# A fifth Strassen pair in the second mixer of a decoder trunk, with a new order of segments and new tables for it

## The chip, the cores and the metric

The kernel runs on one core of one Trainium2 chip. The metric is device time in microseconds of one execution, median over runs; smaller is better. The engines named below are PE (matrix multiplications; PEld is its weight load), DVE (vector), ACT (scalar and activation), POOL and SP (here both used to issue DMAs).

## The reference, cut to what matters

Two layers over 256 rows of 2048 float32 values. Each layer has an attention part and a channel mixer; the mixer, with the norm around it, is what the change touches:

```python
def swiglu(h, w_in, w_out):
    gate, up = jnp.split(h @ w_in, 2, axis=-1)
    return (jax.nn.silu(gate) * up) @ w_out
...
        h = modulate(rms_norm(x, norm_g[layer, 2]), sh2, sc2)
        y = swiglu(h, ffn_w_in[layer], ffn_w_out[layer])
        x = x + g2[:, None, :] * rms_norm(y, norm_g[layer, 3])
```

`w_in` is 2048 x 11264 (gate and up, 5632 columns each), `w_out` 5632 x 2048, and `g2` a vector of 2048 that is itself a product of the condition `c` with a 2048 x 2048 piece of `mod_w`.

## The kernel before

**Products.** Every float32 product is made of three matmuls in the fast `float32r` type: a weight block `raw` (512 x 512, held as 128x2048) is copied in rounded form by ACT (`wh`), DVE subtracts that from the original to get the remainder (`wl`), and PE adds hh·wh, hh·wl and hl·wh into a PSUM bank, where hh and hl are the two parts of the data. A *unit* is one weight block against one half t (128 rows) of the data: 12 matmuls of 128x512. The 5632 inner values are 11 blocks of 512, the 2048 outputs are 4 blocks `nb`.

**A planner.** The Python program keeps its own clock for each engine (`Emit`) and emits instructions when, by its own costs, their inputs will be there: the units stand in a fixed list, weight preparation (`w_load2`, `st_load`) and all epilogues are put between them by the planner. The result is one fixed order per engine; at run time each engine takes its instructions in that order and waits on semaphores. `TUNE` has one row of settings per stage (how many blocks to load ahead, `RAW`; how many prepared weights to keep, `AHEAD` and `MOST`; leads and lateness of preparation and of epilogues); its last row is that of the second mixer. `AT1` is the table of places at which the 16 loads of the last piece of `mod_w` are put among the weight loads. Where the planner expects PE to stand for more than 1.2 (`FILL_MIN`) with a bank free, `fill` emits small matmuls of the identity into a spare bank (`idle`).

**Strassen pairs.** `PAIRS` says how many pairs of inner blocks of each mixer (here one in the first, four in the second) go by Strassen's algorithm in its form with seven products. For a pair p of inner blocks and a pair c of output blocks, the two halves of the rows and the two inner blocks make a 2x2 matrix, which is multiplied by the 2x2 matrix of weight blocks X, Y, W, Z (`st_load`). Plainly that is eight units; here it is seven products, in the order of `ST_ORDER`:

```python
    ST_ADD = {"Q5": ("X", "Y"), "P6": ("X", "Z"), "P7": ("Y", "Z"), "P4": ("X", "W")}
    ST_ORDER = ("P1", "Q5", "P6", "P7", "P3", "P2", "P4")
```

Four of the seven need a weight that DVE first sums in place (`rawX`, `rawY`), and each needs a `wh` and a `wl` of its own. On the data's side `ep_up` keeps the transposed activations of a pair in `fT` (besides their split form `fa`), and `combine` makes the four sums and differences and splits them into `Sh` and `Sl`. After each product `st_out` adds the bank (`sacc`) to the partial output `yp`, on DVE for all pairs but the first.

**Order of the second mixer.** `SEGS` lists, for each mixer, segments of inner blocks: for each block 4 x 2 units of the gate part (`acc` from `hhF`, then `sg` by ACT's Silu) and as many of the up part (DVE multiplies into `sg`, PE transposes into `aT`, ACT and DVE make `fa`). One pair of units, t = 0 and t = 1, shares a weight block. A tuple (p, a, b) in a segment spreads the 14 products of pair p evenly over places a to b in the segment's list of such pairs of units. `LASTK` lists the inner blocks of the last pass: for each output block and each half, `y_block` adds that pass's `acc` to `yp`, ACT sums the squares (`junk`), DVE multiplies by the gate row `G`; `residual` then takes the root (`stat`) and updates X, which goes out. G is a vector of `mod` turned into a row by `gate_rows`: a transposition (`gT`), a copy, a DMA to memory (`grow`) and one back, both on POOL's queue; X comes back from memory by POOL's queue behind it (`x_in`).

Of the kernel before, what the change touches and what calls it, by code (L numbers as in the profile page):

```python
# [50 lines left out]
FILL_FROM = 24.0  # L51
FILL_MIN = 1.2
FILL_LEAVE = 0.7
PAIRS = (1, 4)
W0 = 24
SEGS = (((range(0, 2), (), ()), (range(2, 6), ((0, 3, W0),), range(2, 6)), (range(6, 11), (), ())),
        ((range(0, 2), (), ()), (range(2, 11), ((0, 3, 16), (1, 19, 32), (2, 35, 48), (3, 51, 71)), ())))
LASTK = (range(6, 11), range(8, 11))
ATM = (6, 10, 10, 13, 18, 21, 22, 23, 24, 25, 26, 28, 30, 31, 39, 41, 46, 52, 55, 58, 61, 61, 62, 64, 65, 67, 68, 70,
# [5 lines left out]
AT1 = (1, 4, 4, 4, 6, 7, 33, 46, 60, 73, 95, 112, 115, 126, 139, 149)  # L65

NAMES = ("RAW", "AHEAD", "MOST", "LAG", "LAGX", "LAGR", "T1_LEAD", "URGENT", "LEADS", "BIAS", "ST_RAW", "ST_AHEAD", "XLATE", "LATE", "MLATE", "RLATE")
TUNE = tuple(dict(zip(NAMES, row)) for row in (
# [4 lines left out]

C_ID, C_NTRI, C_ANY, C_NEG1, C_ONE, C_LO, C_HI, C_KEEP = 0, 128, 256, 258, 259, 260, 261, 262
C_MASK, C_MASKT, C_CMP, C_COS, C_SIN, C_END = 262, 390, 518, 550, 806, 1062
# [455 lines left out]
def kernel(ctx: ExitStack, tc, consts, x, c, mod_w, mod_b, norm_g, ffn_w_in, ffn_w_out, a_w_in,  # L531
# [8 lines left out]
    E = Emit(nc)  # L540
# [68 lines left out]
    def cols(n):  # L609
        nstat[0] += n  # L610
        return stat[:, nstat[0] - n:nstat[0]]
# [212 lines left out]
    def w_load2(key, src):  # L824

        st = {}
        view = lambda tl: tl.rearrange("p (j n) -> p j n", j=4)

        def dma():
            st["t"] = E.alloc("pg", "raw")  # L830
            DMA.dma_start(view(st["t"]), src.rearrange("(j p) n -> p j n", p=P))

        def first():
            st["h"] = E.alloc("pg", "wh", R32)
            st["l"] = E.alloc("pg", "wl", R32)
            A.activation(st["h"], st["t"], AF.Copy)

        def second():
            V.tensor_tensor(st["l"], st["t"], st["h"].bitcast(F32), op=OP.subtract)
            E.put("pg", st["t"])  # L840
            E.ready[key] = (view(st["h"]), view(st["l"]), E.fin)

        return Load(key, "w", 2, dma, lambda: E.when(st["t"]), first, second, mid=lambda: E.when(st["h"]))
# [6 lines left out]
    ST_ORDER = ("P1", "Q5", "P6", "P7", "P3", "P2", "P4")  # L850
# [109 lines left out]
    def sumsq(src, acc):  # L960
        j = yield from E.get("s2", "junk")
        A.activation(j, src, AF.Square, accum_out=acc)
        E.put("s2", j)
# [129 lines left out]
    gate_keys = ["A", "F0", "B", "F1"]  # L1093
    PAGED = ["A", "B"] + [f"F{l}" for l in range(2) if PAIRS[l]]
    NEXT = [k for k in ("A", "F0", "B") if gate_keys[gate_keys.index(k) + 1] in PAGED]
# [37 lines left out]
    def y_block(key, nb, t, acc, part=None):  # L1133

        yield from E.wait((key, "G"))
        if nb == 0:
            res[key, t, "ss"] = cols(4)
            res[key, t] = part[t] if part else (yield from E.get("pg", "z"))
        while (key, t) not in res:
            yield False  # L1140
        z = res[key, t][:, nb * NB:(nb + 1) * NB]
        Gb = res[key, "G"][:, nb * NB:(nb + 1) * NB]
        if part:
            V.tensor_tensor(z, acc, z, op=OP.add)
            E.put("mm", acc)
            src = z
        else:
            src = acc
        if part and nb == KT - 1:
            z = res[key, t, "last"] = yield from E.get("s2", "zl")  # L1150
        yield from sumsq(src, res[key, t, "ss"][:, nb:nb + 1])
        V.tensor_tensor(z, src, Gb, op=OP.mult)
        if not part:
            E.put("mm", acc)
        E.flag((key, "y", t, nb))
# [555 lines left out]
    def ep_up(acc, key, blk, t):  # L1711
# [12 lines left out]
        src = b  # L1724
        if blk < 2 * PAIRS[int(key)]:
            src = L["fT" + key, blk, t] = yield from E.get("s2", "fT")
# [7 lines left out]
    def combine(key, p):  # L1734

        yield from E.wait(*[("f" + key, 2 * p + i, t) for i in range(2) for t in range(2)])
        sh = yield from E.get("pg", "Sh", R32)
        sl = yield from E.get("pg", "Sl", R32)
        if p == 0:
            for t in range(2):  # L1740
                ypart[key, t] = yield from E.get("pg", "yp")
        q = [L["fT" + key, 2 * p + i, t] for i in range(2) for t in range(2)]
        v = lambda tl: tl.rearrange("p (q j n) -> p q j n", q=4, j=4)
        sh, sl = v(sh), v(sl)
        flat = lambda tl, i: tl[:, i].rearrange("p j n -> p (j n)")
        for o, a, b, op in ((3, 1, 3, OP.subtract), (1, 0, 1, OP.subtract), (0, 3, 0, OP.subtract), (2, 2, 0, OP.add)):
            V.tensor_tensor(q[o], q[a], q[b], op=op)
            A.activation(flat(sh, o), q[o], AF.Copy)
        yield E.clk["DVE"] - 1.0
        for o in (3, 1, 0, 2):  # L1750
            V.tensor_tensor(flat(sl, o), q[o], flat(sh, o).bitcast(F32), op=OP.subtract)
            E.put("s2", q[o])
        L["S" + key, p] = sh, sl
        E.flag(("S" + key, p))
# [47 lines left out]
    def mm_units(seg, W, col0, nb, kts, lhs, epi, tag="mm"):  # L1802

        us = []
        for i, kt in enumerate(kts):
            key = (seg, nb, kt)
            wsrc[key] = W[kt * NB:(kt + 1) * NB, col0:col0 + NB]
            us.append([dict(kind="mm", key=key, t=t, lhs=(lhs, kt), acc=(seg, nb, t), start=i == 0,
                            stop=i == len(kts) - 1, epi=epi, tag=tag, nb=nb) for t in range(2)])
        return us  # L1810

    def call(fn):
        units.append(dict(kind="call", fn=fn))
# [87 lines left out]
    def ffn_pairs(l, key, gvec, nxt, final):  # L1901
# [7 lines left out]

        for p in range(PAIRS[l]):  # L1910
            call(lambda p=p: E.spawn(combine(key, p)))
# [26 lines left out]
        for nb in range(4):  # L1938
            us = mm_units("y" + key, wo, nb * NB, nb, LASTK[l], fl,
                          lambda a, t, nb_: y_block("F" + key, nb_, t, a, part()))  # L1940
            if nb == 2:
                call(lambda: E.spawn(x_in("F" + key)))
            if nb < 3:
                emit_plain(us)
            else:
                emit_lag(us)

    def ffn_units(l, key, gvec, nxt, final=False):
        if PAIRS[l]:
            return ffn_pairs(l, key, gvec, nxt, final)  # L1950
        lhs = "hF" + key
        fl = "f" + key
        wi, wo = ffn_w_in[l], ffn_w_out[l]

        def in_block(b):
            g = mm_units("g" + key, wi, b * NB, b, range(4), lhs, lambda a, t, nb: ep_gateff(a, key, nb, t))
            u = mm_units("u" + key, wi, DFF + b * NB, b, range(4), lhs, lambda a, t, nb: ep_up(a, key, nb, t))
            return g, u

        for b in range(FB1):  # L1960
            g, u = in_block(b)
            if b == 0:
                emit_lag(g)
                reserve(row("AHEAD"))
            else:
                emit_plain(g)
            emit_plain(u)
        for nb in range(4):
            emit_plain(mm_units("p" + key, wo, nb * NB, nb, range(FB1), fl, lambda a, t, nb_: ep_part(a, key, nb_, t)))
        for b in range(FB1, NFB):  # L1970
            g, u = in_block(b)
            emit_plain(g)
            emit_plain(u)
        reserve(row("LAG") + row("LAGR"))
        part = lambda: [ypart[key, 0], ypart[key, 1]]
        call(lambda: [E.spawn(gate_rows("F" + key, gvec))]
             + [E.spawn(residual("F" + key, t, nxt, final)) for t in range(2)])
        for nb in range(4):
            us = mm_units("y" + key, wo, nb * NB, nb, range(FB1, NFB), fl,
                          lambda a, t, nb_: y_block("F" + key, nb_, t, a, part()))  # L1980
            if nb < 3:
                emit_plain(us)
            else:
                emit_lag(us)
# [31 lines left out]
    def mods_of(vecs):  # L2016
        return [("mod", v, k) for v in vecs for k in range(16)]
# [12 lines left out]
    def placed(ks, mods, at):  # L2030
        assert len(at) == len(mods) and max(at) <= len(ks)
        return [k for i in range(len(ks) + 1) for k in [m for m, a in zip(mods, at) if a == i] + ks[i:i + 1]]
# [14 lines left out]
    ms = mods_of([(1, 5)])  # L2047
    order += placed(ks, ms, AT1)

    for k in order:  # L2050
# [10 lines left out]
        elif k[0] == "st":  # L2061
            E.loads.append(st_load(k))
        elif k in k0[:TWO] or k[0][:-1] in ("g", "u", "y") and PAIRS[int(k[0][-1])]:
            E.loads.append(w_load2(k, wsrc[k]))
# [173 lines left out]
```

## Time and profile before

| | |
|---|---|
| median of 3 runs | 2348.44 us (2348.31 to 2349.58) |
| profiled execution | 2348.64 us, span 2346.9 us |
| PE busy | 2310.0 us, 98% of the span |
| PEld busy | 1880.6 us, 80% |
| DVE busy | 1878.4 us, 80% |
| ACT busy | 1114.1 us, 47% |
| DMA | 672.23 MB, mean 286 GB/s |
| granted PE clock, mean | 0.998 |
| chain that ended last | PE 93%, DVE 2%, ACT 2%, DMA 2% |

Busy time is an average over stages; a stage's own window and its rows tell what it waits for. Matmuls are pipelined, so that the time from one start to the next, not the duration of one, is what a matmul takes. All compute instructions have the line of the recording helper (L130), so rows are told apart by tiles: `sacc` are the Strassen products, `acc` the plain units, `raw` with X, Y, Z or W the weight blocks of a pair. The second mixer runs from 1627.5 us to the end; its last matmul ends at 2338.7.

### The profile page before, as it was taken

Reading aid. Unit: us, or ns where it says so; the run is one execution under the profiler, and the core shown is the slowest. Engines: PE = TensorE matmul, PEld = TensorE weight load, DVE = VectorE, ACT = ScalarE, POOL = GpSimd, SP = SyncE. Lnnn points to the kernel's source line nnn. Section 1 sums busy time; section 2 is a strip of 40 time slices with the busy share of each in tenths; the row PEclk is TensorE's granted clock in tenths of the full one; section 3 lists DMA queues with packets and bytes.
Section 4 is the critical chain, followed back from the end, with each engine's and each line's share of the span. In section 5 each row is a group of like instructions: output and inputs, shape, how many; then the busy total and the mean of one; then the engine's idle time right before and its main releaser. Section 6 shows DMA issues by size and latency. Waiting matters only on the chain.

```text
span 2346.9 us, 27100 instructions
## 1 busy us (share of the span) xinstructions
PE 2310.0 (98%) x10967; PEld 1880.6 (80%) x10967; DVE 1878.4 (80%) x1557; ACT 1114.1 (47%) x1194; POOL 13.1 (1%) x28
## 2 busy tenths in 40 slices
PE   6999999999999999999999999999999999999998
PEld 4678787888888888888888888888888888888887
DVE  4878789997877778877878768886868888888774
ACT  3433555563444334334455355765445445454442
POOL 0000000000000000000000000000000000000000
PEclk9999999999999999999999999999999999999999
DMA  9998977989467999989779979977825666574592
GB/s 352 387 392 308 360 263 292 374 305 338 172 233 279 382 339 389 352 329 333 286 275 337 344 260 363 322 271 274 314 92 204 233 215 233 192 256 164 203 333 107
DMA packets 267646, 672.23 MB, mean 286 GB/s; under 512 B 12672, under 2 KB 30336, under 8 KB 240384
## 3 DMA queue, kind: packets, MB, share of 16 engines
q1 hardware_dynamic: 263808, 649.13, 76.3%
q0 software_dynamic: 3008, 21.01, 2.3%
q8 instruction: 86, 1.41, 0.2%
q10 hardware_dynamic: 704, 0.36, 0.1%
q14 instruction: 40, 0.33, 0.0%
HBM read 662.03 MB, written 8.42 MB: 286 GB/s over the span
## 4 chain that ended last, share of the span: by engine, by line
PE 93%; DVE 2%; ACT 2%; DMA 2%; issue 1%; SPq 0%; DVEq 0%; ACTq 0%
PE acc L130 77%; PE sacc L130 8%; PE sc L130 2%; PE z L130 1%; DVE wl L130 1%; PE oT L130 1%; DMA modq<-in_mod_w_dram 1%; PE aT L130 1%; ACT junk L130 1%; PE pmod L130 1%; PE qacc L130 1%; PE hT L130 1%; ACT hf L130 1%; DMA modw<-in_mod_w_dram 0%; PE cs L130 0%
## 5 line engine op out<-in xcount | busy, mean ns | idle before, releaser
L130 DVE TENSOR_TENSOR wl<-raw,wh 128x2048 fp32r<-128x2048 f32 (+1 forms) x349 | 786.3, 2260 | 169.8 <-ACT wh L130 157.4
L130 ACT ACTIVATE wh<-raw 128x2048 fp32r<-128x2048 f32 (+1 forms) x349 | 658.7, 1893 | 517.0 <-PE acc L130 226.3
L130 PE MATMUL acc<-wh,hhF 128*128 128x512 f32 x2816 | 889.5, 391 | 0.0
L130 PEld LDWEIGHTS acc<-wh,hhF 128*128 128x128 f32 x2816 | 528.5, 188 | 111.4 <-issue 1.7
L130 PE MATMUL acc<-wl,hhF 128*128 128x512 f32 x1408 | 548.0, 389 | 0.0
L130 DVE SCALAR_TENSOR_TENSOR macc<-modw,cact,macc 128x2048 f32<-128x2048 f32 x180 | 422.6, 2348 | 47.2 <-DMA modw<-in_mod_w_dram 37.8
L130 PEld LDWEIGHTS acc<-wl,hhF 128*128 128x128 f32 x1408 | 264.5, 188 | 53.7 <-DVE wl L130 0.2
L130 PE MATMUL acc<-wh,fa 128*128 128x512 f32 x768 | 241.0, 391 | 0.0
L130 PE MATMUL acc<-wh,hA 128*128 128x512 f32 x640 | 220.3, 404 | 1.5 <-DVE hA L130 1.5
L130 PEld LDWEIGHTS acc<-wh,fa 128*128 128x128 f32 x768 | 144.2, 188 | 32.4 <-issue 2.5
L130 PE MATMUL acc<-wh,hhK 128*128 128x512 f32 x512 | 161.2, 392 | 0.4 <-DVE hhK L130 0.4
L130 ACT ACTIVATE wh<-rawX 128x2048 fp32r<-128x2048 f32 x40 | 76.6, 1915 | 156.5 <-DVE rawX L130 137.3
L130 PEld LDWEIGHTS acc<-wh,hA 128*128 128x128 f32 x640 | 120.2, 188 | 37.6 <-issue 13.8
L130 PE MATMUL acc<-wl,fa 128*128 128x512 f32 x384 | 149.6, 390 | 0.0
L130 PE MATMUL acc<-wl,hA 128*128 128x512 f32 x320 | 125.5, 392 | 3.4 <-DVE wl L130 3.4
L130 DVE TENSOR_TENSOR wl<-rawX,wh 128x2048 fp32r<-128x2048 f32 x40 | 91.6, 2290 | 37.9 <-ACT wh L130 37.6
L130 PEld LDWEIGHTS acc<-wh,hhK 128*128 128x128 f32 x512 | 96.0, 188 | 21.2 <-issue 0.8
L130 PE MATMUL acc<-wl,hhK 128*128 128x512 f32 x256 | 99.8, 390 | 0.3 <-DVE wl L130 0.3
L130 PE MATMUL acc<-wh,hhB 128*128 128x512 f32 x256 | 86.5, 400 | 0.0
L130 PE MATMUL acc<-wh,oA 128*128 128x512 f32 x256 | 85.3, 399 | 0.0
L130 PEld LDWEIGHTS acc<-wl,fa 128*128 128x128 f32 x384 | 72.1, 188 | 14.8 <-DVE wl L130 0.3
L130 PE MATMUL acc<-wh,oB 128*128 128x512 f32 x256 | 82.4, 394 | 0.0
(228 smaller groups left out, 2507.6 us busy)
## 6 DMA issues: line engine op xcount, KB each, us to landing
raw<-in_ffn_w_in_dram SPq DMA_DIRECT2D x176, 1024.0 KB, 6.7
modw<-in_mod_w_dram SPq DMA_DIRECT2D x160, 1024.0 KB, 7.0
raw<-in_ffn_w_out_dram SPq DMA_DIRECT2D x48, 1024.0 KB, 7.5
raw<-in_a_w_in_dram SPq DMA_DIRECT2D x40, 1024.0 KB, 14.2
modq<-in_mod_w_dram SPq DMA_DIRECT2D x32, 1024.0 KB, 14.1
modw<-in_kv_mod_w_dram SPq DMA_DIRECT2D x32, 1024.0 KB, 7.5
raw<-in_kv_w_dram SPq DMA_DIRECT2D x32, 1024.0 KB, 9.1
raw<-in_a_w_out_dram SPq DMA_DIRECT2D x16, 1024.0 KB, 8.5
```

Of the source, the lines that this page charges most:

```text
L130: return f(*a, **k)
```

## The change

A fifth pair of inner blocks (8 and 9) of the second mixer goes by the seven products. `LASTK` falls from three blocks to one, block 10. In `SEGS` the products of pairs 0 to 3 stand in narrower stretches (11 places each), and those of pair 4 in places 65 to 71, among the up units of block 9 and the units of block 10. `y_block` is emitted only after all products of its output pair. `AT1` and the last row of `TUNE` have new values.

```diff
-PAIRS = (1, 4)
+PAIRS = (1, 5)
...
-        ((range(0, 2), (), ()), (range(2, 11), ((0, 3, 16), (1, 19, 32), (2, 35, 48), (3, 51, 71)), ())))
-LASTK = (range(6, 11), range(8, 11))
+        ((range(0, 2), (), ()), (range(2, 11), ((0, 3, 14), (1, 19, 30), (2, 35, 46), (3, 51, 62), (4, 65, 71)), ())))
+LASTK = (range(6, 11), range(10, 11))
...
-AT1 = (1, 4, 4, 4, 6, 7, 33, 46, 60, 73, 95, 112, 115, 126, 139, 149)
+AT1 = (1, 4, 4, 4, 12, 19, 32, 39, 44, 60, 72, 83, 87, 101, 103, 122)
...
-    (6, 2, 5, 6, 2, 0, 3, (9, 3, 0), (8.0, 0, 10.0), (-0.9, 0.2, -1.0), 4, 4, (0.3, 0.6), 3.8, 0.5, 0.7)))
+    (6, 2, 4, 6, 2, 0, 3.5, (9, 7, 0), (19.0, 19.0, 24.0), (-0.5, 0.2, -0.9), 4, 4, (0.4, 0.9), 1.6, 0.5, 1.5)))
...
     def y_block(key, nb, t, acc, part=None):
 
         yield from E.wait((key, "G"))
+        if part:
+            l = int(key[1])
+            yield from E.wait(*[("so" + key[1], p, nb // 2, nm) for p in range(PAIRS[l]) for nm in ST_ORDER])
```

Up to the second mixer the order of every engine is that of before. Within it, three places are shown. First DVE, where it prepares the second column pair of the last pair of blocks. Before (that pair is the fourth) the rows from the first product's weight to the third's are, with `raw` without a letter a plain block:

```order
L130 TENSOR_TENSOR wl_15252<-rawX_15203,wh_15251 128x2048
L130 TENSOR_TENSOR wl_15283<-raw_15215,wh_15282 128x2048
L130 TENSOR_TENSOR rawX_15203<-rawX_15203,rawY_15243 128x2048
L130 TENSOR_TENSOR wl_15313<-rawX_15203,wh_15312 128x2048
L130 TENSOR_TENSOR yp_12284<-yp_12284,sacc_15316 128x512
L130 TENSOR_TENSOR wl_15331<-raw_15289,wh_15330 128x2048
L130 TENSOR_TENSOR rawX_15203<-rawX_15203,rawZ_15338 128x2048
L130 TENSOR_TENSOR yp_12300<-yp_12300,sacc_15363 128x512
L130 TENSOR_TENSOR wl_15377<-rawX_15203,wh_15376 128x2048
```

and now (the fifth):

```order
L130 TENSOR_TENSOR wl_15801<-rawX_15726,wh_15800 128x2048
L130 TENSOR_TENSOR yp_12272<-yp_12272,sacc_15635 128x512
L130 TENSOR_TENSOR rawX_15726<-rawX_15726,rawY_15728 128x2048
L130 TENSOR_TENSOR wl_15839<-rawX_15726,wh_15838 128x2048
L130 TENSOR_TENSOR rawX_15726<-rawX_15726,rawZ_15808 128x2048
L130 TENSOR_TENSOR yp_12271<-yp_12271,sacc_15858 128x512
L130 TENSOR_TENSOR yp_12272<-yp_12272,sacc_15879 128x512
L130 TENSOR_TENSOR wl_15875<-rawX_15726,wh_15874 128x2048
L130 TENSOR_TENSOR rawY_15728<-rawY_15728,rawZ_15808 128x2048
L130 TENSOR_TENSOR wl_15893<-raw_15823,wh_15892 128x2048
```

The plain splits that stood between the summed ones are gone from these rows.

Second PE at the third product (P6) of that column pair. Before it is followed and preceded by plain units without a filler; now:

```order
L130 MATMUL sacc_15879<-wh_15838,Sl_15594 128x512
L130 LDWEIGHTS identb
L130 MATMUL idle_15901<-identb 128x256
...
L130 MATMUL sacc_15858<-wh_15874,Sh_15593 128x512
L130 LDWEIGHTS identb
L130 MATMUL idle_15911<-identb 128x256
...
L130 MATMUL sacc_15858<-wl_15875,Sh_15593 128x512
L130 MATMUL sacc_15858<-wh_15874,Sl_15594 128x512
```

Eight fillers stand ahead of P6's first matmul and thirteen ahead of its second, which is the first to read `wl`; nine stand behind the first matmul of the next plain unit, and nine in the last pass. The second mixer had none before.

Third PE where the last pass begins, `hhF` being block 10's up units and `fa` the activations of a block. Before (three blocks in that pass):

```order
L130 MATMUL acc_15628<-wh_15702,hhF_1769_11586 128x512
L130 MATMUL acc_15795<-wh_15721,fa_15069 128x512
L130 MATMUL acc_15795<-wl_15722,fa_15069 128x512
...
L130 MATMUL aT_15815<-K,sg_15595 128x128 x4
L130 MATMUL acc_15823<-wh_15721,fa_15069 128x512
...
L130 MATMUL aT_15839<-K,sg_15613 128x128 x4
L130 MATMUL acc_15795<-wh_15739,fa_15439 128x512
```

and now (block 10 alone):

```order
L130 MATMUL acc_15845<-wh_16042,hhF_1769_11586 128x512
L130 MATMUL gT_16122<-K,mall 16x128
L130 MATMUL aT_16129<-K,sg_15773 128x128 x4
L130 MATMUL acc_16137<-wh_16058,fa_16134 128x512
L130 MATMUL acc_16137<-wl_16059,fa_16134 128x512
...
L130 MATMUL aT_16157<-K,sg_15791 128x128 x4
L130 MATMUL acc_16168<-wh_16058,fa_16134 128x512
```

Before, the two transpositions of block 10 stood among units of earlier blocks; now the unit behind the first of them reads what it makes, and the gate row's `gT` stands just ahead of it. On DVE the last pass has the same rows but one order: the four updates of X for t = 0 stand directly ahead of the last add of t = 1 in both, with one unit of PE between the two halves' last matmuls instead of three.

## The prediction

> **What bounds the kernel now.** I read the page's head, then the stretch of the second mixer as one window, then the chain that ended last, then DVE and ACT in order of time where the change puts its new work.
>
> ```profile
> span 2346.9 us, 27100 instructions
> PE 2310.0 (98%) x10967; PEld 1880.6 (80%) x10967; DVE 1878.4 (80%) x1557; ACT 1114.1 (47%) x1194; POOL 13.1 (1%) x28
> PE 93%; DVE 2%; ACT 2%; DMA 2%; issue 1%; SPq 0%; DVEq 0%; ACTq 0%
> 1627.50:2338.70 711.20, 711.08 (x3190) 587.00 (x3188) 564.04 (x401) 342.95 (x264) 2.66 (x5) 1.00 0.61 217
> 1867.73 5.44 PE sacc L130 x24
> ```
>
> The window from 1627.5 to 2338.7 is the second mixer, from its first matmul to its last: columns are PE, PEld, DVE, ACT, POOL, then the granted clock 1.00. PE is busy 711.08 of 711.20 us, so in this stage it waits for nothing, and a matmul taken out there is worth its full spacing. The row of the chain gives that: 24 matmuls take 5.44 us, 0.2267 us each; a unit (12 matmuls, one block against one half of the rows) takes 2.72 us. DVE is busy 79% of the stage. So every microsecond that PE learns to wait here is lost as fully as a matmul is won.
>
> **What is removed.** Two units of eight go to seven products for each of two column pairs: 24 matmuls, 5.44 us. Nothing else can be won in this stage, since there is no wait to take away. The profiled execution took 2348.64 us, 1.7 us more than its span; the median of the runs is 2348.44, so the same sum from either differs by 0.2 us.
>
> By the Trainium skill, "TensorE: Matmul & The Clock Gate", section Back-to-back issue gap, matmuls of 512 columns in a stream with weight loads come about 131 ns apart, by which the 24 would be worth about 3.1 us (an estimate). The row has 227 ns; the measurement decides.
>
> **What is added, on DVE and ACT.** The durations, in order of time:
>
> ```profile
> 2085.64 2.28 DVE L130 TENSOR_TENSOR rawX<-rawX,rawW 128x2048 f32<-128x2048 f32 x1
> 2089.96 2.29 DVE L130 TENSOR_TENSOR wl<-rawX,wh 128x2048 fp32r<-128x2048 f32 x1 [2.04 <-ACT wh L130]
> 2092.17 0.68 DVE L130 TENSOR_TENSOR yp<-yp,sacc 128x512 f32<-128x512 f32 x1
> 2092.77 2.28 DVE L130 TENSOR_TENSOR wl<-raw,wh 128x2048 fp32r<-128x2048 f32 x1
> ...
> 2103.36 0.43 DVE L130 CAST fa<-fT 128x512 fp32r<-128x512 f32 x1
> 2103.82 0.69 DVE L130 TENSOR_TENSOR fa<-fT,fa 128x512 fp32r<-128x512 f32 x1
> 2104.43 2.29 DVE L130 TENSOR_TENSOR wl<-raw,wh 128x2048 fp32r<-128x2048 f32 x1
> 2106.63 2.86 DVE L130 TENSOR_TENSOR fT<-fT,fT 128x512 f32<-128x512 f32 x4
> 2109.41 2.35 DVE L130 SCALAR_TENSOR_TENSOR macc<-modw,cact,macc 128x2048 f32<-128x2048 f32 x1
> 2111.67 2.49 DVE L130 TENSOR_TENSOR Sl<-fT,Sh 128x512 fp32r<-128x512 f32 x4
> 2114.08 2.29 DVE L130 TENSOR_TENSOR wl<-rawX,wh 128x2048 fp32r<-128x2048 f32 x1
> ```
>
> From start to start: a 128x2048 instruction takes 2.20 us, a 128x512 one 0.60, a cast 0.46, the four of combine's sums 2.78, its four remainders 2.41. The first two rows show the weak spot: a product with a summed weight needs an add on DVE, the rounded copy `wh` on ACT, then the remainder `wl` on DVE, and DVE stands 2.04 us for ACT if it has nothing in between.
>
> A pair trades 8 weight splits for 14 and adds 8 sums, so 14 instructions of 2.20 us more, about 31 us of DVE, with combine's 5.2 and the output sums on top. Blocks two to four have it in cycles of 46 units, 125 us of PE, and there DVE has, counted in the order, 30 splits, 8 sums, 2 to 4 `macc` (2.26 us), 6 to 14 output sums and some 20 small ones: by these rows 106 to 112 us in the new order against 103 to 108 before, beside PE as today. The `macc` of the last gate vector now all come in these cycles, none behind them: they add to the 112, and take 2.26 us each out of what follows. I cost the narrower bunches (11 pairs instead of 13 for 14 products) at nothing, covered by the five pairs of plain units behind each; 3 us if that cover fails.
>
> The fifth pair has no such rest behind it. I walk DVE's new order from T0, the end of the second transposition of block 9 (aT into PSUM), by those durations. DVE reaches the work of that half at T0+1.3: it has two products with `sg`, one add, a copy, a cast, a remainder and a split (7.45 us together) from the last-but-one unit of block 9, while PE has two units and two transpositions (6.15 us). From there to the remainder that block 10's first half needs stand 29 instructions of 2.20 (63.8 us) and 16.6 us of small ones (two of a cast, 2.78, 2.41, 14 output sums, two `sg`, one more). DVE also stands behind the add, copy, remainder sequence six times, with whatever small work is left to fill it: 1.2 + 0.35 (the first of them for P1's end on PE), 1.5, 2.1, 2.1, 0.9 and 1.5 us, 9.65 in all. 1.3 + 63.8 + 16.6 + 9.65: that remainder ends at T0+91.3.
>
> PE has 29 units up to there, 78.9 us, one small transposition and block 10's first aT, then two matmuls before the one that needs the remainder:
>
> ```profile
> 2273.18 0.60 PE L130 MATMUL aT<-K,sg 128*128 128x128 f32 x4
> ...
> 2273.54 0.48 PE L130 MATMUL acc<-wh,fa 128*128 128x512 f32 x1
> ...
> 2274.77 0.60 ACT L130 ACTIVATE fa<-aT 128x512 fp32r<-128x512 f32 x1 [2.42 <-DVE wl L130]
> ```
>
> That is 78.9 + 0.1 + 0.36 + 0.45 = T0+79.75 if PE never waits. PE waits 11.7 us, by the walk 0.35 before P6, 1.2 P7, 0.7 P4 and 0.1 the next unit (column pair 0), 1.2 before Q5, 1.7 and 2.05 at P6, 1.7 in the unit behind it (column pair 1), 0.7 for ACT's `fa` and 2.0 for its remainder. The second half adds 0.4: 12.1 us. Before, block 10's aT went under four units of blocks 8 and 9 that the last pass had first; now that pass has block 10 alone.
>
> The 39 filler matmuls that now stand at four of these places are no more than part of the waits. Alone they would cost:
>
> ```profile
> 1236.74 2.58 PE L130 MATMUL idle<-identb 128*128 128x256 bf16 x22
> ```
>
> 0.117 us each, 4.6 us, even if PE would not have waited.
>
> **The end.** The last output block of each half of the rows:
>
> ```profile
> 2319.69 0.69 DVE L130 TENSOR_TENSOR yp<-acc,yp 128x512 f32<-128x512 f32 x1 [5.81 <-PE acc L130]
> 2321.18 0.69 DVE L130 TENSOR_TENSOR yp<-yp,G 128x512 f32<-128x512 f32 x1 [0.79 <-ACT junk L130]
> ...
> 2324.50 0.15 DVE L130 TENSOR_REDUCE stat<-stat 128x1 f32<-128x3 f32 x1
> ...
> 2324.94 0.15 DVE L130 TENSOR_SCALAR stat<-stat 128x1 f32<-128x1 f32 x1
> ...
> 2330.57 0.69 DVE L130 TENSOR_TENSOR yp<-acc,yp 128x512 f32<-128x512 f32 x1 [5.48 <-PE acc L130]
> ...
> 2334.57 0.75 DVE L130 SCALAR_TENSOR_TENSOR X<-zl,stat,X 128x512 f32<-128x512 f32 x1
> 2338.73 0.69 DVE L130 TENSOR_TENSOR yp<-acc,yp 128x512 f32<-128x512 f32 x1 [3.41 <-PE acc L130]
> ```
>
> From the first half's last add to the end of its four updates of X DVE needs 4.75 us; three units, 8.16 us, lay between the two halves, so the second never met the first. Now one unit, 2.72 us, lies between, and the four small sums of `stat` (0.6 us from the first to the last's end) fall into the same place, in front of the square root: the second half starts 5.3 us behind the first instead of 2.7, 2.6 us later.
>
> The gate row G comes late:
>
> ```profile
> 2288.24 0.50 POOL L130 DMA_DIRECT2D grow<-grow  x1 [650.61 <-ACT grow L130]
> 2293.77 0.56 POOL L130 DMA_DIRECT2D G<-grow  x1 [5.02 <-DMA raw<-in_ffn_w_out_dram]
> ...
> 2298.80 0.69 DVE L130 TENSOR_TENSOR yp<-yp,G 128x512 f32<-128x512 f32 x1 [3.91 <-DMA G<-grow]
> ```
>
> 10.6 us from its first DMA to its use. The new order issues it when the last pass begins, about T0+88.9, so the first output block waits until T0+99.5. DVE then takes 2.1 us a block (1.49 from add to product in the first two rows above, and 0.60), PE 2.72. PE's eight units of that pass end at T0+113.3 (91.4, the rest of the first unit with an aT 2.6, 0.4 of wait, seven units 19.0), and DVE has caught up by then: nothing, and a microsecond for each that G is later than that. X stands behind G on POOL and is used ten us later; the weight loads on SP go out at least 15 us ahead of use: nothing for these.
>
> **The sum.** -5.44 + 12.1 + 2.6 = +9.3 us: 2357.9 for the profiled execution, 2357.7 for the median. Bounds: only the fillers and the end, -5.44 + 4.6 + 2.6, 2350.2; all four bunches (3) and G (3) on top, 2363.7. I take the walk, since each of its durations is a row of the same stage.
>
> **The rivals.** First, not slower: DVE keeps further ahead than I have it at T0, so that PE waits only where the fillers stand. It decides at the last pair: below 7.5 us of waits the change is within 0.2%, and at the fillers' 4.6 it is 2350.2. For it speaks that PE waits nowhere in this stage today; against it, that the walk starts at a transposition which DVE cannot run ahead of. Second, the bunches and G cost what I left out: 2361 to 2364. DVE's 79% of the stage speaks against it, G's 3.91 us of wait for it. Third, the clock falls behind the waits. In this stage it was granted in full throughout, with PE never idle, so no row here shows what a pause of 2 us does; three such pauses within 9 us, and then the unit behind one or two of them at half speed (2.7 us each), give 2360 to 2363. By the Trainium skill, the same page, Part 1, the gate halves the clock after an idle window of about 3.4 us, and each such window would cost 1.7 us (an estimate); my longest wait is 2.05. Fourth, faster: it needs waits and end together below 0.7 us, and the fillers alone are 4.6.
>
> **How the numbers follow.** My forecast 0.65, the first rival 0.12, the second 0.15, the third 0.05, the fourth 0.03. A measurement of this kernel can tell about 0.2%, 4.7 us, from no change: slower 0.85, same 0.12, faster 0.03. The range 2351.5 to 2363.5 leaves out part of the first rival and the top of the second.
>
> **What would show it.** Right: PE busy short of the stage by about 12 us, waits on `wl` at sacc and acc rows in the last 130 us and none before; DVE over 90% there; the last add of the second half following the first half's update of X at once, and 10 to 11 us from the last matmul to the end instead of 8.2 (2338.7 to 2346.9). Wrong: PE rows without gaps around the last pair's second column pair, or gaps in the first four bunches too.

## The result, and the profile after

The changed kernel takes 2370.53 us (median of four runs, 2369.51 to 2372.00) against 2348.38 us before: a ratio of 1.0093, 95% interval 1.0081 to 1.0105. It is slower, as forecast, but by 22.2 us where 9.3 were forecast, outside the stated range. The profiled execution took 2369.56 us. Its head, the chain that ended last, and the second mixer from its first matmul to its last:

```profile
span 2367.8 us, 27171 instructions
PE 2313.1 (98%) x10982; PEld 1878.7 (79%) x10982; DVE 1922.1 (81%) x1591; ACT 1131.0 (48%) x1210; POOL 13.1 (1%) x28
PE 17%; DVE 5%; issue 2%; ACT 2%; DMA 0%; DVEq 0%; ACTq 0%
1627.50:2357.30 729.80, 715.21 (x3207) 585.25 (x3205) 605.11 (x432) 360.40 (x281) 2.66 (x5) 1.00 0.59 211
```

The mixer lasts 729.4 us instead of 711.2 (its first matmul starts at 1627.91, 0.4 us into the window); PE is busy 714.8 of them (fillers count as busy), and the chain, PE for 93% of the span before, is followed back only to 1747.9 us now, with DVE and ACT in it. What PE waited for in the mixer, summed by what came last (us, times, longest; the five largest rows):

```profile
PE sacc L130 <- DVE yp L130: 7.3, 3, 2.6
PE sacc L130 <- DVE wl L130: 3.7, 6, 1.0
PE sacc L130 <- ACT yp L130: 1.4, 1, 1.4
PE acc L130 <- ACT fa L130: 0.7, 1, 0.7
PE sacc L130 <- ACT wh L130: 0.7, 1, 0.7
```

The first and third rows are a kind of wait that the prediction does not have: a product waits until an earlier product has been added to the output. They lie in the first four bunches, where I had none. The mixer cut in two, before and then after (the columns are those of the windows in the prediction):

```profile
1640.00:2240.00 600.00, 600.00 (x2688) 496.49 (x2687) 490.97 (x332) 293.56 (x206) 0.00 (x0) 1.00 0.61 214
2240.00:2338.70 98.70, 98.69 (x445) 80.35 (x443) 63.34 (x53) 41.00 (x39) 2.12 (x4) 1.00 0.58 212
```

```profile
1640.00:2240.00 600.00, 590.57 (x2645) 486.37 (x2644) 498.75 (x335) 298.01 (x213) 0.00 (x0) 1.00 0.62 220
2240.00:2357.33 117.33, 112.28 (x506) 88.78 (x505) 96.86 (x82) 53.81 (x49) 2.12 (x4) 1.00 0.40 144
```

PE loses 9.4 us in the first 600 us, in which it lost nothing before. One of these places, PE first and then DVE:

```profile
1935.65 0.39 PE L130 MATMUL sacc<-wh,Sl 128*128 128x512 f32 x1
1938.66 0.47 PE L130 MATMUL sacc<-wh,Sh 128*128 128x512 f32 x1 [2.62 <-DVE yp L130]
```

```profile
1931.31 2.28 DVE L130 TENSOR_TENSOR rawY<-rawY,rawZ 128x2048 f32<-128x2048 f32 x1
1935.62 2.29 DVE L130 TENSOR_TENSOR wl<-rawY,wh 128x2048 fp32r<-128x2048 f32 x1 [2.03 <-ACT wh L130]
1937.83 0.68 DVE L130 TENSOR_TENSOR yp<-yp,sacc 128x512 f32<-128x512 f32 x1
```

The matmul at 1935.65 is P6's last, the one at 1938.66 is P7's first. P7 adds on top of P6 in the same bank, so it may not start before P6's content has been added to `yp`. That add is one instruction of DVE, and DVE had just begun a remainder, for which it had stood 2.03 us waiting for ACT; the add comes 2.2 us later and P7 another 0.83 us after the add's start. The remainder is that of P7's own weight, `rawY`. In the kernel before, PE has two plain units between the two products, and DVE does both instructions meanwhile, in the other order (PE: P6's last matmul, the first plain one, P7's first; then DVE):

```profile
1939.04 0.39 PE L130 MATMUL sacc<-wh,Sl 128*128 128x512 f32 x1
1939.27 0.39 PE L130 MATMUL acc<-wh,hhF 128*128 128x512 f32 x1
...
1944.71 0.39 PE L130 MATMUL sacc<-wh,Sh 128*128 128x512 f32 x1
```

```profile
1939.47 0.69 DVE L130 TENSOR_TENSOR yp<-yp,sacc 128x512 f32<-128x512 f32 x1
1941.44 2.29 DVE L130 TENSOR_TENSOR wl<-rawY,wh 128x2048 fp32r<-128x2048 f32 x1 [1.28 <-ACT wh L130]
```

Why there? A bunch puts product i of a pair at place a + (b - a) i / 14, ahead of the next whole place. Over 11 places (19 to 30) P6 and P7 of the second column pair fall on 26.07 and 26.86: nothing stands between them. Over 13 (19 to 32) they fall on 27.36 and 28.29, with two plain units between. The first four bunches all have this; the fifth, 65 to 71, has not.

Where the 20.9 us between the two profiled executions went; each gap is the distance of the two matmuls' starts around it less the normal 0.227 us (above: 3.01 - 0.23 = 2.78), with the 0.1 us by which the next start is late behind it, fillers included:

| | us | forecast |
|---|---|---|
| 24 matmuls fewer | -5.4 | -5.4 |
| P7 behind P6, four bunches: 1.68, 2.86, 2.86, 2.28 | +9.7 | 0 |
| other gaps in these bunches | +1.3 | 0 |
| around the fifth pair: 0.56, 1.23, 0.72, 6.68 | +9.2 | +9.0 |
| last pass, block 10's activations | +3.45 | +3.1 |
| last matmul to the end: 10.4 instead of 8.2 | +2.3 | +2.6 |
| ahead of the second mixer, where the programs agree | +0.4 | |

The three terms that I worked out came within half a microsecond. The fifth pair's second column pair, which the prediction walks through, and the last pass:

```profile
2292.76 0.50 PE L130 MATMUL sacc<-wl,Sh 128*128 128x512 f32 x1 [0.85 <-DVE wl L130]
2295.39 1.05 PE L130 MATMUL idle<-identb 128*128 128x256 bf16 x8
2297.09 0.50 PE L130 MATMUL sacc<-wh,Sh 128*128 128x512 f32 x1 [0.65 <-ACT wh L130]
2297.43 1.59 PE L130 MATMUL idle<-identb 128*128 128x256 bf16 x13
2299.41 0.50 PE L130 MATMUL sacc<-wl,Sh 128*128 128x512 f32 x1 [0.39 <-DVE wl L130]
...
2303.82 0.50 PE L130 MATMUL acc<-wl,hhF 128*128 128x512 f32 x1 [0.39 <-DVE wl L130]
...
2332.53 0.50 PE L130 MATMUL acc<-wh,fa 128*128 128x512 f32 x1 [0.69 <-ACT fa L130]
2334.59 0.73 PE L130 MATMUL acc<-wh,fa 128*128 128x512 f32 x2 [0.32 <-DVE fa L130]
```

A wait still stands behind each group of fillers, so these cost nothing here. And the end, where the second half's add follows the first half's update of X at once:

```profile
2354.65 0.69 DVE L130 TENSOR_TENSOR yp<-acc,yp 128x512 f32<-128x512 f32 x1 [0.55 <-PE acc L130]
...
2358.94 0.74 DVE L130 SCALAR_TENSOR_TENSOR X<-zl,stat,X 128x512 f32<-128x512 f32 x1
2359.60 0.68 DVE L130 TENSOR_TENSOR yp<-acc,yp 128x512 f32<-128x512 f32 x1
```

So the theory to test was: P6 and P7 back to back cost the 9.7 us (A). Its rivals: narrow bunches overload DVE wherever the products stand (B); the new settings make DVE late (C).

### The profile page after: what moved, and what is told of

The parts are those of the page before. It is cut to its first block, busy times and chain, and to the rows that moved or that the text cites. A ratio compares the mean times of both kernels' runs of the same rounds, so it can differ in the third digit from the quotient of the medians.

```text
span 2367.8 us, 27171 instructions
## 1 busy us (share of the span) xinstructions
PE 2313.1 (98%) x10982; PEld 1878.7 (79%) x10982; DVE 1922.1 (81%) x1591; ACT 1131.0 (48%) x1210; POOL 13.1 (1%) x28
## 5 line engine op out<-in xcount | busy, mean ns | idle before, releaser
L130 DVE TENSOR_TENSOR wl<-raw,wh 128x2048 fp32r<-128x2048 f32 (+1 forms) x341 | 767.5, 2259 | 165.3 <-ACT wh L130 155.4
L130 ACT ACTIVATE wh<-raw 128x2048 fp32r<-128x2048 f32 (+1 forms) x341 | 642.4, 1892 | 491.0 <-PE acc L130 212.6
L130 PE MATMUL acc<-wh,fa 128*128 128x512 f32 x640 | 201.4, 392 | 1.1 <-ACT fa L130 0.7
L130 ACT ACTIVATE wh<-rawX 128x2048 fp32r<-128x2048 f32 x48 | 91.9, 1916 | 186.5 <-DVE rawX L130 180.8
L130 PEld LDWEIGHTS acc<-wh,fa 128*128 128x128 f32 x640 | 120.0, 188 | 28.7 <-issue 1.7
L130 DVE TENSOR_TENSOR wl<-rawX,wh 128x2048 fp32r<-128x2048 f32 x48 | 109.9, 2290 | 38.0 <-ACT wh L130 37.5
L130 PE MATMUL acc<-wl,fa 128*128 128x512 f32 x320 | 124.7, 390 | 0.6 <-DVE wl L130 0.6
L130 PE MATMUL sacc<-wh,fa 128*128 128x512 f32 x288 | 94.3, 389 | 0.0
L130 PE MATMUL sacc<-wh,Sh 128*128 128x512 f32 x192 | 75.5, 393 | 9.3 <-DVE yp L130 7.3
```

What stands on the lines that cost most here:

```text
L130: return f(*a, **k)
```

## The experiments

| | median us | ratio to before, 95% interval |
|---|---|---|
| x1_shift | 2366.91 | 1.0077 (1.0064 to 1.0089) |
| x2_narrow4 | 2365.68 | 1.0076 (1.0064 to 1.0089) |
| x3_set4 | 2352.04 | 1.0015 (1.0006 to 1.0024) |
| x4_nofill | 2372.95 | 1.0106 (1.0090 to 1.0121) |
| x5_wide5 | 2363.81 | 1.0067 (1.0054 to 1.0079) |
| x6_late | 2366.03 | 1.0077 (1.0063 to 1.0091) |
| x7_nosum | 2362.76 | 1.0056 (1.0043 to 1.0068) |
| x8_tail | 2371.48 | 1.0098 (1.0084 to 1.0112) |
| x9_nosum5 | 2358.90 | 1.0045 (1.0033 to 1.0058) |
| x10_p3mid | 2368.47 | 1.0084 (1.0071 to 1.0098) |
| x11_spread | 2361.41 | 1.0054 (1.0042 to 1.0067) |
| x12_adj | 2365.71 | 1.0077 (1.0064 to 1.0089) |

**The adjacency alone, in the kernel before.**

```diff
-at = [(a + (b - a) * i / 14.0, u) for ...
+at = [(a + (b - a) * (10 if l and i == 9 else i) / 14.0, u) for ...
```

> The kernel before (four pairs, wide bunches, its own settings) with one thing moved: P6 of the second column pair goes directly ahead of P7, four times in the program. Theory A: 1.0 us each if only the way over DVE's output sum counts, 1.5 to 2.8 if DVE stands behind its sums there as in the changed trace: 2348.5 + 4 to 11. Rival (narrow bunches cost by DVE's load in them, not by the adjacency): within 1.5 us of 2348.5.

It cost 17 us, more than either theory gave. The trace has four waits of PE for the add of P6, 3.14, 3.13, 2.70 and 2.26 us, and no other. The second of them, on PE, and the window behind it:

```profile
1954.46 0.77 PE L130 MATMUL sacc<-wh,Sh 128*128 128x512 f32 x1 [3.14 <-DVE yp L130]
1955.02 0.63 PE L130 MATMUL sacc<-wl,Sh 128*128 128x512 f32 x1
```

```profile
1954.00:1960.50 6.50, 6.04 (x15) 4.77 (x16) 5.26 (x4) 2.90 (x2) 0.00 (x0) 0.52 0.49 161
```

The granted clock in the window is 0.52, and fourteen matmuls come 0.43 us apart instead of 0.227. That is 2.8 us on top of the wait. It happened behind both waits over 3 us and, for 1.7 us, behind the one of 2.26; not behind the one of 2.70. So in this execution the four gaps cost 11.9 us, the half clock 7.3, and 2.3 more lie ahead of the mixer, where the programs agree. It is the slowest of five, which lie between 2363.7 and 2370.3 us; such losses could explain the spread, though only this one has a trace. A is shown: four pairs, wide bunches, old settings, and one product moved.

**The same adjacency by narrow bunches, old settings.**

```diff
-((0, 3, 16), (1, 19, 32), (2, 35, 48), (3, 51, 71))
+((0, 3, 14), (1, 19, 30), (2, 35, 46), (3, 51, 62))
```

> The kernel before (four pairs, its own settings) with nothing changed but the places of the bunches, which are those of the changed kernel (3 to 14, 19 to 30, 35 to 46, 51 to 62). Theory A: P6 and P7 of the second column pair are back to back four times, so PE waits 1.5 to 2.8 us four times: 2348.4 + 6 to 11, about 2357. Rival C (the new settings, and not the places): no change, 2348 to 2350. The planner puts fillers at three of the four places, which lie within the wait.

17 us again, not the 9 expected. The gaps at P7 and its remainder are 3.57, 3.52, 3.79 and 3.78 us with their fillers, and 1.7 us of half clock stand behind the first. At the other three the add does not wait. In the second it starts as soon as P6 has ended, and PE then stands for the copy and the remainder of P7's own weight (P7 starts at 1942.03, its second matmul at 1944.35):

```profile
1940.91 0.69 DVE L130 TENSOR_TENSOR yp<-yp,sacc 128x512 f32<-128x512 f32 x1 [0.94 <-PE sacc L130]
1942.01 2.29 DVE L130 TENSOR_TENSOR wl<-rawY,wh 128x2048 fp32r<-128x2048 f32 x1 [0.40 <-ACT wh L130]
```

So the add ahead of the remainder did not help here: back to back, both stand between P6 and P7. C is out as the main cause: the old settings do worse here.

**The settings alone**, in the kernel before: the new row of `TUNE` and the new `AT1`.

> The kernel before (four pairs, its own places) with only the new settings row and the new table of loads of the last gate vector. Theory A: within 1.5 us of 2348.4, since P6 and P7 are never adjacent. A wait of about 0.9 us like the one at 2094 us of the changed trace, where DVE stood for a load of that vector, may show. Rival C (the settings make DVE late in the bunches): about +8, 2356.

3.3 us slower, twice what I allowed: gaps of 0.3 to 0.9 us, five in all, nearly all where PE waits for a remainder. So settings made for five pairs have a price of their own, in bunches that did not wait before. Row and table were not run apart. For the gap at 1817 us the traces point to the table: a `macc` of 2.34 us now stands at 1807.01, ahead of the sum for P7's weight, and the same `macc` and gap are in x5 and in x11, which has the old row, but not in the kernel before.

**The bunches moved by 0.3 of a place.**

```diff
-(0, 3, 14), (1, 19, 30), (2, 35, 46), (3, 51, 62)
+(0, 3.3, 14.3), (1, 19.3, 30.3), (2, 35.3, 46.3), (3, 51.3, 62.3)
```

> The changed kernel with the first four bunches moved by 0.3 of a place, at the same width of 11 (3.3 to 14.3, 19.3 to 30.3, 35.3 to 46.3, 51.3 to 62.3). In the changed kernel P6 and P7 of the second column pair stand back to back in each of these bunches, and its trace has waits of 1.41, 2.62, 2.62 and 2.04 us there (P7's first matmul, for the output sum of P6, which reads the bank that P7 adds to). The shift puts two plain units between them. Theory A (back to back P6 and P7): these waits go, 1.6 + 2.8 + 2.8 + 2.2 = 9.4 us over the normal spacing, and the time falls from 2370.5 to about 2361. Rival B (too many products for DVE in a narrow bunch, wherever they stand): the waits come back at other products, 2368 to 2371. Rival C (the settings make DVE late): as B.

The waits for the add are gone, but only 3.6 us came back. In their place stand waits for remainders; in the whole mixer PE now waits for (the three largest rows):

```profile
PE sacc L130 <- DVE wl L130: 4.7, 9, 1.0
PE sacc L130 <- ACT wh L130: 1.1, 2, 0.6
PE acc L130 <- DVE wl L130: 0.9, 2, 0.5
```

The gaps of the four bunches sum to 7.2 us here, fillers included, against 11.0. B holds too, then.

**P3 between P6 and P7**, at the same narrow width.

```diff
+    ST_ORDER1 = ("P1", "Q5", "P6", "P3", "P7", "P2", "P4")
+    ST_FREE1 = {"P7": "YZ", "P4": "XW"}
...
```

> The changed kernel with the products of the second mixer in the order P1, Q5, P6, P3, P7, P2, P4: in the narrow bunches P3 now follows P6 at once, and P7 never does. The third weight block of a pair is held one product longer. Theory A: the four waits at P7 (9.5 us) go, some of it comes back as waits for remainders, as in the shifted bunches (7.2 us there): 2364 to 2367. Rival (each narrow bunch has its waits wherever the products stand): 2369 to 2371.

Between the two: 2368.47. No wait for an add is left, and the bunches cost some 7 us as in the shifted kernel; the fifth pair and the last pass went from 12.6 to 15 us (whether because P3's block is held longer is not shown).

**Wide bunches.**

```diff
-(0, 3, 14), (1, 19, 30), (2, 35, 46), (3, 51, 62), (4, 65, 71)
+(0, 3, 16), (1, 19, 32), (2, 35, 48), (3, 51, 64), (4, 65, 71)
```

> The changed kernel with the first four bunches 13 places wide (3 to 16, 19 to 32, 35 to 48, 51 to 64): P6 and P7 are never adjacent and products have the spacing of the kernel before. The narrow bunches cost 11.0 us over the normal spacing in the changed trace. Theory D (narrowness itself, by adjacency and by DVE's load in it): the first three bunches lose their waits (1.7, 2.8, and 2.8 + 1.0), while the fourth now ends one place ahead of the fifth, which takes the rest that DVE had between them: two more waits of about 2 us there. 2370.5 - 11.0 + 4.5 = 2364, 2361 to 2366. Rival C (settings): the waits in the first three bunches stay, 2369 or more.

As expected, 2363.81:

```profile
1640.00:2240.00 600.00, 598.22 (x2680) 492.36 (x2678) 503.57 (x347) 296.00 (x213) 0.00 (x0) 1.00 0.63 220
```

The first four bunches keep some 3 us, the size of what the settings alone cost, with gaps at 1818, 2007 and 2016 us where x3 has them too. At 2246 to 2258 us, where the fourth bunch now meets the fifth, 6.0 us are lost instead of 1.8. The 11.0 us of the narrow bunches thus come apart: about 3 remain with wide ones (settings), 4 more when narrow without adjacency (B), and 4 more with it (A). A's own gaps are larger than that (9.7): without them part of the time comes back as waits for remainders, as in the shifted kernel.

**The fifth pair without its weight sums.**

```diff
-            if nm in ST_ADD:
+            if nm in ST_ADD and p < 4:
...
```

> The changed kernel without DVE's eight weight sums of the fifth pair (it uses the weights as they were; the products of that pair are then other numbers). DVE has 8 x 2.20 = 17.6 us less in the last 110 us and no sum, copy, remainder sequence. If DVE's work sets the waits there, as in the prediction, the 9.2 us around the last pair go nearly all and those of the last pass in part: 10 to 12 us less, 2359 to 2361, with the four earlier bunches unchanged. If it were the chain of products over one bank, the waits would stay: 2368 or more.

Around the fifth pair no gap is left (9.2 before), and the last pass lost 2.2 us instead of 3.45. In the stretch from 2240 us to the last matmul PE is idle 0.7 us:

```profile
2240.00:2350.57 110.57, 109.87 (x497) 90.17 (x495) 82.72 (x77) 53.24 (x48) 2.12 (x4) 1.00 0.45 158
```

So DVE's work is what sets those waits. The time missed its range by 1.8 us; this execution had 1.7 us of half clock behind the second bunch's wait and a 1.7 us wait for a remainder at 2092.

**No weight sums in all five pairs.**

```diff
-            if nm in ST_ADD:
+            if nm in ST_ADD and lay == 0:
...
```

> The changed kernel without DVE's weight sums in all five pairs of the second mixer (the products of the pairs are then other numbers). P6 and P7 of the second column pair stay back to back in the first four bunches; DVE has 8 x 2.20 us less in each. It splits the 2.6 us waits there: if adjacency alone is what costs, the floor is the way of P6's output sum (DVE's add is 0.69 us, with the hand-overs on both sides about 1 us), so four waits near 1 us stay; if it was DVE standing behind the sum, copy, remainder sequence, what is over 1 us goes. Theory A with both: x7 (2362.8, sums left out in the fifth pair alone) less 4 x 1.5 and the 2 to 3 us of the waits for remainders: about 2354 to 2356. Rival (adjacency does not matter, DVE's load alone): no wait stays, 2350 to 2351.

P7's waits are 2.30, 2.31 and 2.30 us in the three bunches whose add DVE makes, and 0.69 in the first, whose add ACT makes. Not the sum chain, then, but any 2.2 us instruction in front of the add (here P7 starts at 1936.90):

```profile
1933.87 2.29 DVE L130 TENSOR_TENSOR wl<-rawZ,wh 128x2048 fp32r<-128x2048 f32 x1 [0.98 <-ACT wh L130]
1936.08 0.68 DVE L130 TENSOR_TENSOR yp<-yp,sacc 128x512 f32<-128x512 f32 x1
```

My floor of 1 us would need DVE to be free; 0.69 is the nearest measured. Two stretches of half clock (1.7 us each) are part of the miss too. By the Trainium skill, "TensorE: Matmul & The Clock Gate", Part 1 (Architectural detail), ScalarE and VectorE take their instructions strictly in order; each of these traces agrees, the add never passing the remainder.

**No fillers in the second mixer.**

```diff
-n = int(...) if t - t0 > FILL_MIN else 0
+n = int(...) if t - t0 > FILL_MIN and self.stage < 3 else 0
```

> The changed kernel without the 39 filler matmuls of the second mixer. If they lie inside waits, as I forecast: 2369.5 to 2371, and the waits named in the trace grow by what the fillers took. If they cost their own time (39 x 0.117 us): 4.6 us less, 2366.

Neither: it is 2.4 us slower. The second column pair of the fifth pair and the last pass, where the fillers stood, lose 12.5 us in this trace instead of 10.1, since the clock falls there when PE is silent. Two windows:

```profile
1937.00:1941.00 4.00, 3.03 (x7) 2.48 (x8) 4.00 (x4) 2.44 (x2) 0.00 (x0) 0.58 0.61 197
2300.00:2306.00 6.00, 5.17 (x12) 4.12 (x13) 5.25 (x4) 2.66 (x3) 0.00 (x0) 0.50 0.66 250
```

The second row stands behind two waits of 1.54 and 1.83 us around P6 of the fifth pair. The first row is a place that has fillers in neither kernel: the same wait of 2.62 us halves the clock here and does not in the changed kernel's trace. The same happens 1.4 us behind P7's wait in the third bunch. In the last pass the clock falls too, from 2337.0 to 2340.4, behind waits of 0.69 and 1.32 us.

**The fifth pair's last products later.**

```diff
-(4, 65, 71)
+(4, 65.3, 74)
...
-            assert not at
+            units.extend(u for _, u in at)
```

> The changed kernel with the products of the fifth pair at 65.3 to 74 instead of 65 to 71, the last four behind all units of block 10's up part, ahead of the last pass. The changed trace lost 9.2 us around this pair and 3.4 us where the last pass waits for block 10's activations. Theory E (the order of the last 100 us leaves PE without cover at two places): the four products cover block 10's transposition, and the wider bunch halves the rest: 5 to 8 us less, 2363 to 2366. Rival F (DVE has as much work as PE there, and no order helps): the waits move and stay in sum, 2369 to 2372.

2366.03, at the edge of E: the gaps around the fifth pair and the last pass fall from 12.6 to 5.4 us. But the last pass then begins with DVE behind, and the end takes 12.1 us from the last matmul instead of 10.4; this trace has 1.7 us of half clock as well. E holds for the waits and F for a part of what they turn into.

**The last two output blocks interleaved.**

```diff
+                for t in range(2):
+                    units.extend([held[0][t], us[0][t]])
...
```

> The changed kernel with the last two output blocks interleaved: third block first half, fourth block first half, then both for the second half, so that two units instead of one lie between the halves' last matmuls. The time from the last matmul to the end was 8.2 us before and 10.65 in the changed trace. If it is the update of X for the first half that stands in front of the second half's last add, about 2.4 us come back: 2368. If not, 2370.5.

Missed: 2371.48. From the last matmul to the end it is 10.0 us, 0.4 less. The second half's third block now stands behind the first half's update as well, and its 2.1 us of DVE take what the wider distance gave. That the update stands in front of the add is plain in both traces; that it can be had cheaper is not shown.

**Five pairs with all of it.** Wide bunches without adjacent P6 and P7, the late fifth pair, the old row of `TUNE` (the new `AT1` stays), G ahead of the last pass.

```diff
-(0, 3, 14), (1, 19, 30), (2, 35, 46), (3, 51, 62), (4, 65, 71)
+(0, 3, 16), (1, 19, 32), (2, 34.5, 47.5), (3, 49.6, 61.6), (4, 65.3, 74)
...
```

> Five pairs with what the runs so far point to: bunches 13 wide without adjacent P6 and P7 (3 to 16, 19 to 32, 34.5 to 47.5, 49.6 to 61.6), the fifth at 65.3 to 74 with its last four products behind block 10's up units, the settings row of before, and the gate row G made before the last pass. The sum: 2348.5 - 5.4 for the matmuls, 1 to 3 for the first four bunches, 5 to 7 around the fifth (5.4 measured in the late variant), 2 to 4 for the end: 2352 to 2357, still not faster than before. If DVE's work of five pairs can be hidden by order at all, it is under 2348.

2361.41, the best of the complete five-pair kernels and still 13 us behind; my sum was 4 too low. Its waits are for remainders:

```profile
PE sacc L130 <- DVE wl L130: 4.9, 10, 0.8
PE acc L130 <- DVE wl L130: 1.7, 1, 1.7
PE sacc L130 <- ACT wh L130: 0.3, 1, 0.3
```

With fillers the gaps sum to 8 us in the first four bunches, 7 of them in the third and fourth, which stand closer behind the bunch ahead now (that this is the reason is not shown), and to 7 around the fifth. No version beat the kernel before.

## Why the prediction failed, point by point

- *24 matmuls, 5.44 us*: as forecast; with it the sum above closes.
- *The walk from T0, 12.1 us of waits*: 12.6 measured. The second column pair alone, 1.2 + 1.7 + 2.05 + 1.7, came as 6.68, and leaving out the eight sums took nearly all of it away, so the reason was right with the size. That the total came within half a microsecond is in part luck: by the walk's own durations its small items sum to 16.3, not 16.6, and PE's side to 79.8, so it should have given 0.3 to 0.4 us less.
- *The end, 2.6 us*: 2.3, with the row that I named.
- *G and the other loads at nothing*: G's first DMA went out at 2331.79 and its first use at 2339.74 waited for ACT alone, 8.0 us later, where the walk took 10.6. Right.
- *The narrower bunches "at nothing, covered by the five pairs of plain units behind each; 3 us if that cover fails"*: this is the step that failed. They cost 11.0 us. It argued with DVE's load over a cycle of 125 us (106 to 112). But P7 waits for certain instructions of DVE, the add of P6 and the remainder of its own weight, and what counts is what of them is left when P6 ends: here a 2.2 us remainder ahead of the add, mean load or not. The rows to see it lay in the order of PE, which I had read for the fifth pair only; the arithmetic of the places shows it too. Of the 11, 4 go when P6 and P7 are pulled apart, 4 more when the bunches are wide again, which is load indeed, and the 3 left are most likely the settings, which I had not costed at all.
- *Second rival, bunches and G late, 2361 to 2364*: right place for the bunches, wrong size, and for a reason that it did not name; G was not late.
- *Third rival, the clock*: the mechanism is real, though the profiled execution of the changed kernel shows a clock of 1.00 throughout the mixer; it appears in six of the variants. I had tied it to three pauses of 2 us around the fifth pair, and there the fillers hold it off: without them 2.4 us more are lost.
- *First rival, not slower, and fourth, faster*: PE stood in more places than the fillers did, so both fell.
- *The signs*: the late add of the second half and the 10 to 11 us at the end came, as did a sign of being wrong, gaps in the first four bunches. DVE over 90% did not: it is busy 96.86 of the last 117.33 us, 83%.

## What to carry to other kernels

A chain of matmul groups that accumulate in one bank, with a vector add of the bank between them, needs other matmuls between two links: back to back, each link with an add on DVE cost 2.0 to 3.1 us of waiting in the changed kernel and in x12 (DVE 83% busy over the mixer of the first), and 3.5 to 3.8 with the weight in x2. When work is spread by a formula, list which pairs fall on the same place before any load is averaged. Where a wait cannot be had away, small matmuls in it were worth more than they cost here: 2.4 us by the medians with and without them.

## What the runs showed of the hardware that was not expected

The granted clock halves after short pauses: seen after single waits of 2.26 to 3.14 us, after 1.54 and 1.83 us in a row, and after 0.69 and 1.32 (x4), with matmuls 0.43 us apart for 7 to 14 of them (1.4 to 2.8 us lost). The same wait of 2.62 us did it in some executions and not in others. Each stretch lasts 3.4 us or twice that: the granted clock is 0.50 from 1936.88 to 1940.29 in x9 and from 1953.37 to 1960.19 in x12. By the Trainium skill, the same page, Part 1, the gate looks at a free-running window of about 3.4 us; the dependence on chance agrees with that, but waits of 2.3 us were enough, so one pause need not fill such a window.
